# A hybrid encoder block on one core: a sum of squares moves to VectorE, a read-out goes ahead of a product, a down product starts by tile pairs, and two first loads change queues

## The chip, the core and the metric

The kernel runs on one core of a Trainium2 chip. The core has five engines, each with an instruction stream of its own that it works off in order: TensorE (PE) multiplies matrices and writes to the PSUM banks, VectorE (DVE), ScalarE (ACT) and GpSimd (POOL) work element by element, and SyncE (SP) issues loads and stores. ACT issues some of the loads too. Engines wait for one another through semaphores. The metric is the time of one execution on the device in microseconds (us). Of several runs the median counts.

## What is computed

One layer with 1024 tokens of width 1024, float32:

```python
h = rms_norm(x, norm1_g[l])
z = h @ w_in[l]
a, gate, q, k, v = jnp.split(z, splits, axis=-1)
conv_out = conformer_conv(a, gate, dw_kernel[l], dw_bias[l], conv_ln_g[l], conv_ln_b[l])
...
attn_out = neighbourhood_attention(q, k, v, rpb[l])
mix = jnp.concatenate([conv_out, attn_out], axis=-1)
x = x + mix @ w_out[l]
h = rms_norm(x, norm2_g[l])
x = x + (jax.nn.silu(h @ w_gate[l]) * (h @ w_up[l])) @ w_down[l]
```

`conformer_conv` multiplies `a` by the sigmoid of `gate`, runs a 31-tap convolution over positions for each of 512 channels, normalises over the channels (mean, then the mean of the squared deviations, which is the sum of squares in the change) and applies silu. The neighbourhood attention has 8 heads of 64. The inner width of the last line is 2816.

## The kernel before

**Precision.** Every large product is made of three matmuls: each operand is split into a rounded part (`hi`, a cast on ACT) and the remainder (`lo`, a subtraction on DVE or POOL; `split`, L107 to L113), and `mac` (L115 to L119) adds hi x hi, hi x lo and lo x hi into one PSUM bank. L117, L118 and L119 of the profile are these three; they work on 512 columns mostly.

**Order.** The schedule is written out by hand: each engine executes its instructions in the order in which the code records them. PE's products are recorded one by one; `weave` (L127) is called after a product and records the next waiting piece of side work, so a number in `slots` (L1012) says after how many products a piece stands in the streams.

**First loads (L243 to L266).** `chunks` is the list of weight pieces to load; `issue` (L142) issues the next one on SP. The first piece is `wk0`, 128 x 1024, in two halves: the first is loaded by ACT (L258), the second by the first call of `issue`. The token tiles `xt00` to `xt03` (two blocks of 128 rows by 512 tokens each) are loaded in two halves of tokens, FIRST and SECOND, by `load_xt` (L244). ACT's queue holds wk0's first half, xt00's SECOND half and `par` (small parameters); SP's holds xa, xt00's FIRST half, wk0's second half, xt01's FIRST half, wk1 and so on. A load's data is cast by ACT and split by DVE before PE reads it. The products z of the first four token tiles run over these weights: `first_two` (L581) takes wk0's two blocks for tiles 0 and 1, first block, then second, then tiles 2 and 3 follow, which need xt00's SECOND half, then wk1.

**The convolution's normalisation (L890 to L937).** For each half h of the tokens: `conv_mean` sums over channels on PE; `conv_dev` subtracts the mean from the four channel blocks on DVE (L899), squares each on ACT (L901), adds the first two squares on POOL (L903) and the other two and then the sums on DVE (L904, L905); `conv_var` transposes that sum on PE (L910), reduces it on DVE (L911), takes the root on ACT (L912) and the reciprocal on DVE (L913); `conv_rows` spreads the result over the partitions; `conv_norm` (L930) and `conv_silu` make the normalised blocks `cm` (with a `split`, L113), which PE's output projection reads as `pj<-cm`. The pieces of the second half (h = 1) stand at slots 4 (deviation), 13 (variance), 18 and 19, woven into the attention part of the output projection.

**Gate and up (L1300 to L1500).** For each of 22 blocks i of the inner width, gate and up for both halves of the tokens are computed together by a 2 x 2 block scheme with seven products m1 to m7 in place of eight. Each ends in a PSUM bank, and `evac` (L1348) reads it out. Gate's silu for the first half of the tokens is `sl`; for the second half it is left in the bank `D` by m4's read-out (`gate2`, L1340). Two products finish up: m3's read-out adds m3 to the rest (L1369), multiplies the sum with `sl` (L1370) and stores it (`keep`); for the second half, `up2` (L1344) multiplies bank D with up's other sum (L1345) and stores that. `up2` waits in the list `late` after m4 and is recorded behind the read-out of the next product, which is m3 (L1493). Bank D comes from a pool of two banks, so the D of the next block cannot be written before `up2` has read an older one. Some of the blocks' m1 and m2 are themselves split in four by the same scheme (`part`); their banks are q40, q41 and q42 in the rows below.

**Down (L1509 to L1596).** The same scheme for the last product: `SEQ` (L1402) gives the order m1, m2, m6, m5, m7, m3, m4, each over 11 blocks k of the inner width and four tiles t of 128 output columns. m6 and m5 use the banks GB (B0d, B1d, and two halves of a larger tile that both read B2d in the profile), and m5 goes on adding where m6 ended. After the last k of m6 each tile is read out on DVE by `finish` (L1546), tiles 2 and 3 last. Operands of a block (`op`) are prepared four blocks ahead by `prep_item`: two casts on ACT, two subtractions on DVE; one buffer holds two blocks.

Of the kernel before, what the change touches and what calls it, by code (L numbers as in the profile page):

```python
# [9 lines left out]
OP = mybir.AluOpType  # L10
# [61 lines left out]
def build(ctx, tc, a):  # L72
# [66 lines left out]
    def want(src, name, dst, sub=(pool,)):  # L139
        chunks.append((src, name, dst, sub))  # L140

    def issue():  # L142
        if pos[0] < len(chunks):
            src, name, _, _ = chunks[pos[0]]
            if pos[0] not in raws:
                raws[pos[0]] = R(name + "r")
            d = raws[pos[0]]
            if len(src.shape) == 3:
                d = d.rearrange("p (k m) -> p k m", k=src.shape[1])
            sl = slice(512 if name == "wk0" else 0, None)  # L150
            nc.sync.dma_start(d[:, sl], src[:, sl])
            pos[0] += 1

    def take(n=1, ahead=True):
# [86 lines left out]
        x_t[t] = G(f"x{t}")  # L241
        nc.sync.dma_start(x_t[t], a["x"][t * P:(t + 1) * P, :])

    def load_xt(h, kp, sl, queue=None):  # L244
# [3 lines left out]
        (queue or nc.sync).dma_start(xr[h, kp][:, ks, sl], a["xt"][h, kp][:, ks, sl])  # L248

    xr[0, 0] = G("xt00").rearrange("p (k s) -> p k s", s=512)  # L250
    raws[0] = R("wk0r")
# [4 lines left out]
    xa = ST("xa")[:, :258]  # L256
    nc.sync.dma_start(xa, a["xa"])
    nc.scalar.dma_start(raws[0][:, :512], chunks[0][0][:, :512])  # L258
    load_xt(0, 0, SECOND, nc.scalar)
    nc.scalar.dma_start(par, a["par"])  # L260
    for kp in range(4):
        load_xt(0, kp, FIRST)
        if kp < 3:
            issue()
        if kp > 0:
            load_xt(0, kp, SECOND)  # L266
    g1 = par[:, 0:8]
    dwk = par[:, 8:132].rearrange("p (c t) -> p c t", t=CW)
    dwb, lng, lnb = par[:, 132:136], par[:, 136:140], par[:, 140:144]
# [625 lines left out]
    def conv_dev(h):  # L895
        sq = []
        for c in range(4):
            w = of(c, h)
            dve.scalar_tensor_tensor(w, cw["m", h], -1.0 / 512, w, OP.mult, OP.add)  # L899
            sq.append(ST(f"sd{h}{c}"))  # L900
            act.activation(sq[c], w, AF.Square)  # L901
            if c == 1:
                pool.tensor_tensor(sq[0], sq[0], sq[1], OP.add)  # L903
        dve.tensor_tensor(sq[2], sq[2], sq[3], OP.add)  # L904
        dve.tensor_tensor(sq[0], sq[0], sq[2], OP.add)  # L905
        cw["s", h] = sq[0]
# [47 lines left out]
    for i in range(4, 32, 2):  # L954
# [31 lines left out]
        if jobs:  # L986
# [23 lines left out]

    cm += [half(f"cm{h}") for h in range(2)]
    slots = {0: lambda: (weigh(31), evac_hi(7), evac_lo(7)), 3: lambda: conv_var(0),  # L1012
             4: lambda: (conv_mean(1), conv_dev(1)), 6: lambda: (conv_rows(0), conv_norm(0, 0)), 13: lambda: conv_var(1),
             18: lambda: conv_rows(1),
             19: lambda: (act.activation(warm, eps, AF.Silu), [conv_norm(0, c) for c in (1, 2, 3)],
                          conv_silu(0, 0), conv_norm(1, 0))}
# [331 lines left out]
    def evac(i, p, acc):  # L1348
        if p == "m1":
            gt[i] = G(f"g{i}")  # L1350
        l, r = lr(gt[i])
        if p == "m1":
            act.copy(l, acc)
        elif p == "m6":
            u2[i] = ST(f"u2{i}")
            dve.tensor_tensor(u2[i], acc, l, OP.add)
            if i < 2:
                gate2(i, bank[i, "D"])
        elif p == "m2":
            sl[i] = ST(f"sl{i}") if i < 4 else acc  # L1360
            if parted(i, "m1"):
                dve.tensor_tensor(acc, acc, l, OP.add)
            act.activation(sl[i], acc, AF.Silu)
        elif p in ("m5", "m7"):
            dve.tensor_tensor(r, acc, l if p == "m7" else r, OP.add)  # L1365
            if i < 2 and p == "m5":
                up2(i, r, bank[i, "D"])
        elif p == "m3":
            dve.tensor_tensor(l, acc, l, OP.add)  # L1369
            dve.tensor_tensor(l, sl[i], l, OP.mult)  # L1370
            keep(i, 0, l)
        elif i > 1:
            gate2(i, acc)
            late.append(lambda: up2(i, r, acc))
# [110 lines left out]
    for n, (i, p) in enumerate(products):  # L1485
        if n == 1:
            woven.extend([lambda: token_sums(1), lambda: None, lambda: None, lambda: token_rows(1)])
        pacc = product(i, p)
        evac(i, p, pacc)
        if n in after:  # L1490
            after[n]()
        if late and p != "m4":
            late.pop(0)()  # L1493
        due = extra and p in ("m2", "m5", "m7", "m6", "m3")[:5 if parted(i, "m2") else 4]
        if due and not parted(i, "m1"):
            extra.pop(0)()
# [12 lines left out]
        if i == FB - 1 and p in ("m5", "m4", "m3"):  # L1509
            prep_items(1 + (p == "m5"))  # L1510
# [103 lines left out]
```

## Time and profile before

| | |
|---|---|
| runs | 1020.76, 1021.34, 1021.4 us, median 1021.34 |
| the profiled execution | 1020.85 us, of which 1018.9 is the span from its first to its last instruction |
| DVE busy | 782.1 us, 77% of the span |
| ACT busy | 476.5 us, 47% |
| POOL busy | 458.4 us, 45% |
| TensorE's granted clock | 1.0 throughout |
| chain of waits that ended last | TensorE 96%, DVE 1%, POOL 1% |

The profile gives for each engine when an instruction began and how long it took. A row of the time line reads: start, duration, engine, line of the kernel, operation, output <- inputs by the program's names, shapes, count of instructions merged into the row, and in brackets how long the engine had been idle before and what ended that. PE overlaps its matmuls, so their durations overlap too and the distance between two starts is what one costs. The waits of an engine are listed as: who waited <- for whom, total us, times, longest.

### The profile page before, as it was taken

What the parts mean: (1) busy time and instruction counts of PE and PEld (TensorE: products, weight loads), DVE (VectorE), ACT (ScalarE), POOL (GpSimd) and SP (SyncE); (2) the same over time, 40 slices, a digit from 0 to 9 for tenths busy, and PEclk for the clock granted to TensorE, in tenths of its full rate; (3) what the DMA queues carried; (4) which work ended last, traced back from release to release, by engine and by line L of the source; (5) the groups of instructions that cost most, each with busy time, mean ns of one, the idle gap of its engine ahead of it and who ended that gap; (6) DMA issues with size and microseconds to landing.
All of it is one profiled execution on the core that took longest, in us unless ns stands there. A gap on an engine that the chain in (4) does not pass through costs nothing.

```text
span 1018.9 us, 15107 instructions
## 1 busy us (share of the span) xinstructions
PE 1013.9 (100%) x5258; PEld 848.2 (83%) x5258; DVE 782.1 (77%) x1227; ACT 476.5 (47%) x1042; POOL 458.4 (45%) x386
## 2 busy tenths in 40 slices
PE   9999999999999999999999999999999999999998
PEld 8888888877788888888888888888888888888887
DVE  5788997896768476988887787777777766768874
ACT  7556357837877245433433343343332443443432
POOL 1036684535663466266556567566665200003200
PEclk9999999999999999999999999999999999999999
DMA  9416682236503620124334344343341796634631
GB/s 351 169 49 221 204 241 85 96 109 211 179 23 134 238 94 32 58 99 153 137 118 150 126 141 137 119 153 125 135 134 63 255 364 233 211 104 134 213 119 42
DMA packets 75756, 151.70 MB, mean 149 GB/s; under 512 B 14472, under 2 KB 23560, under 8 KB 75040
## 3 DMA queue, kind: packets, MB, share of 16 engines
q1 hardware_dynamic: 73392, 147.12, 42.9%
q10 hardware_dynamic: 2288, 3.62, 1.0%
q8 instruction: 42, 0.69, 0.3%
q14 instruction: 34, 0.28, 0.1%
HBM read 112.06 MB, written 44.11 MB: 153 GB/s over the span
## 4 chain that ended last, share of the span: by engine, by line
PE 96%; DVE 1%; POOL 1%; DMA 0%; ACT 0%; issue 0%; SPq 0%; POOLq 0%; DVEq 0%; ACTq 0%
PE B L117 6%; PE B L118 6%; PE B L119 6%; PE z L117 4%; PE z L119 4%; PE z L118 4%; PE D L117 4%; PE D L118 4%; PE D L119 4%; PE gl L119 3%; PE gl L118 3%; PE gl L117 3%; PE pj L117 3%; PE pj L118 3%; PE pj L119 3%; PE p L779 2%
## 5 line engine op out<-in xcount | busy, mean ns | idle before, releaser
L382 DVE SCALAR_TENSOR_TENSOR cv<-u,par,cv 128x1009 f32<-128x1009 f32 (+14 forms) x92 | 117.5, 1277 | 2.3
L409 POOL TENSOR_TENSOR pa<-pa,pr 128x1022 f32<-128x1022 f32 (+5 forms) x24 | 58.0, 2416 | 38.0 <-ACT pr L408 37.5
L1557 POOL TENSOR_TENSOR ou<-ou,resm 128x512 f32<-128x512 f32 x8 | 12.4, 1553 | 138.4 <-DVE ou L1548 126.1
L109 ACT CAST op<-sr 128x512 fp32r<-128x512 f32 x77 | 47.7, 619 | 57.1 <-PE B2d L119 26.7
L113 DVE TENSOR_TENSOR op<-sr,op 128x512 fp32r<-128x512 f32 x77 | 57.6, 748 | 17.5 <-ACT op L109 17.4
L109 ACT CAST op<-wd 128x512 fp32r<-128x512 f32 x54 | 33.4, 619 | 30.3 <-DVE wd L1452 19.2
L757 ACT ACTIVATE e<-e,mx 128x341 f32<-128x341 f32 (+5 forms) x64 | 35.3, 553 | 18.1 <-DVE mx L752 18.1
L768 POOL TENSOR_SCALAR e<-e,rs 128x341 f32<-128x341 f32 (+5 forms) x64 | 32.9, 528 | 22.1 <-DVE rs L766 21.6
L113 DVE TENSOR_TENSOR op<-wd,op 128x512 fp32r<-128x512 f32 x54 | 40.2, 745 | 1.6 <-ACT op L109 0.4
L1104 DVE TENSOR_TENSOR ts<-gu,ts 128x512 f32<-128x512 f32 x36 | 40.5, 1126 | 0.6
L752 DVE CUSTOM_DVE_ANT_0 e<-s,tab 128x341 f32<-128x341 f32 (+5 forms) x64 | 27.2, 481 | 13.1 <-PE s L735 12.9
L1365 DVE TENSOR_TENSOR g<-D,g 128x512 f32<-128x512 f32 x22 | 15.2, 689 | 23.0 <-PE D L119 23.0
L436 ACT ACTIVATE sq<-z,r 128x64 f32<-128x64 f32 x96 | 28.3, 330 | 5.1 <-PE z L119 5.1
L1342 ACT ACTIVATE D<-D 128x512 f32<-128x512 f32 x22 | 12.8, 582 | 35.7 <-DVE D L1341 35.7
L408 ACT ACTIVATE pr<-u,par 128x1022 f32<-128x1022 f32 (+5 forms) x24 | 27.0, 1137 | 1.6 <-ACT vs L466 1.6
L117 PE MATMUL B2d<-op 128*128 128x512 f32 x66 | 25.8, 391 | 0.0
L119 PE MATMUL B2d<-op 128*128 128x512 f32 x66 | 25.7, 390 | 0.0
L118 PE MATMUL B2d<-op 128*128 128x512 f32 x66 | 25.7, 389 | 0.0
L779 PEld LDWEIGHTS p<-ident,e 128*128 128x128 f32 (+1 forms) x184 | 19.7, 135 | 6.7 <-POOL e L768 5.1
L1058 POOL TENSOR_TENSOR sq<-sq,sq 128x512 f32<-128x512 f32 x12 | 17.6, 1468 | 16.5 <-ACT sq L1054 16.3
L779 PE MATMUL p<-ident,e 128*128 128x128 f32 (+1 forms) x184 | 23.9, 277 | 0.0
L735 PE MATMUL s<-kT,qT 64*128 64x341 f32 (+5 forms) x128 | 21.6, 452 | 0.2
(1492 smaller groups left out, 3752.9 us busy)
## 6 DMA issues: line engine op xcount, KB each, us to landing
gu<-in_gu SPq DMA_DIRECT2D x44, 512.0 KB
sr<-sd SPq DMA_DIRECT2D x77, 256.0 KB
sd<-sd SPq DMA_DIRECT2D x22, 512.0 KB
wd<-in_wd SPq DMA_DIRECT2D x36, 256.0 KB
sd<-g SPq DMA_DIRECT2D x33, 256.0 KB
x<-in_x SPq DMA_DIRECT2D x8, 512.0 KB
xT<-in_xp SPq DMA_DIRECT2D x8, 512.0 KB
xd<-xT SPq DMA_DIRECT2D x16, 256.0 KB
```

The lines of the kernel that those rows point to most:

```text
L109: act.copy(hi, src)
L113: eng.tensor_tensor(*[w[..., sl] for w in (lo, src, hi.bitcast(F32))], OP.subtract)
L117: pe.matmul(acc, lh, rh, start=start, stop=False, skip_group_check=True)
L118: pe.matmul(acc, lh, rl, start=False, stop=False, skip_group_check=True)
L119: pe.matmul(acc, ll, rh, start=False, stop=stop, skip_group_check=True)
L382: dve.scalar_tensor_tensor(acc[:, o], uc[:, i], dwk[:, c, t:t + 1], acc[:, o], OP.mult, OP.add)
L409: pool.tensor_tensor(pa[:, o], pa[:, o], pr[:, o], OP.add)
L436: act.activation(sq[:, h * HD:(h + 1) * HD], z[:, h * HD:(h + 1) * HD], AF.Square, scale=r, accum_out=ss[:, h:h + 1])
L757: act.activation(e, e, AF.Exp, bias=mx.pop((i, hh)), scale=-1.0, accum_out=sums[i][:, hh:hh + 1])
L768: pool.tensor_scalar(es[i][:, hh], es[i][:, hh], rs[:, hh:hh + 1], 1.0, op0=OP.mult, op1=OP.mult)
L779: pe.transpose(pt[:m, g * P:(g + 1) * P], et[i][:, hh, k.start:k.start + m], ident)
L1104: (pool if (i, n) in ON_POOL else dve).tensor_tensor(o, l, r, OP.subtract)
```

## The change

Four edits.

First loads: `issue` can be given a queue. wk0's second half is issued on ACT, behind the first; xt00's SECOND half is issued on SP, behind its FIRST half.

```diff
-    def issue():
+    def issue(queue=None):
...
-            nc.sync.dma_start(d[:, sl], src[:, sl])
+            (queue or nc.sync).dma_start(d[:, sl], src[:, sl])
...
     nc.scalar.dma_start(raws[0][:, :512], chunks[0][0][:, :512])
-    load_xt(0, 0, SECOND, nc.scalar)
+    issue(nc.scalar)
     nc.scalar.dma_start(par, a["par"])
     for kp in range(4):
         load_xt(0, kp, FIRST)
-        if kp < 3:
+        if 0 < kp < 3:
             issue()
-        if kp > 0:
-            load_xt(0, kp, SECOND)
+        load_xt(0, kp, SECOND)
```

Convolution: for the second half of the tokens the first two squares are added on DVE instead of POOL, after all four deviations, and the variance stands at slot 12 instead of 13.

```diff
-            if c == 1:
+            if (h, c) == (0, 1):
                 pool.tensor_tensor(sq[0], sq[0], sq[1], OP.add)
+        if h == 1:
+            dve.tensor_tensor(sq[0], sq[0], sq[1], OP.add)
         dve.tensor_tensor(sq[2], sq[2], sq[3], OP.add)
         dve.tensor_tensor(sq[0], sq[0], sq[2], OP.add)
...
-             4: lambda: (conv_mean(1), conv_dev(1)), 6: lambda: (conv_rows(0), conv_norm(0, 0)), 13: lambda: conv_var(1),
+             4: lambda: (conv_mean(1), conv_dev(1)), 6: lambda: (conv_rows(0), conv_norm(0, 0)), 12: lambda: conv_var(1),
```

Gate and up: m3's product with the gate, and its store, go to the end of `late`, and the whole list is recorded at once, so `up2` comes first.

```diff
         elif p == "m3":
             dve.tensor_tensor(l, acc, l, OP.add)
-            dve.tensor_tensor(l, sl[i], l, OP.mult)
-            keep(i, 0, l)
+            late.append(lambda: (dve.tensor_tensor(l, sl[i], l, OP.mult), keep(i, 0, l)))
...
-        if late and p != "m4":
+        while late and p != "m4":
             late.pop(0)()
```

Down: m5's first two blocks k run on tiles 0 and 1 first, then on tiles 2 and 3.

```diff
-            n = s * QF + k
-            for t in range(4):
-                down(n, t)
+            ahead = p == "m5" and k < 2
+            for k_, t in [(k_, t) for k_ in (0, 1) for t in (2 * k, 2 * k + 1)] if ahead else [(k, t) for t in range(4)]:
+                down(s * QF + k_, t)
```

What the streams hold before and after, at three places. Lines behind L143 are numbered one or two differently after the change. DVE in the convolution's second half (mr1 is the mean, u0 to u3 the channel blocks, sd10 to sd13 their squares), before and then after:

```order
L899 SCALAR_TENSOR_TENSOR u3_1306<-mr1_3339,u3_1306 128x512
L904 TENSOR_TENSOR sd12_3350<-sd12_3350,sd13_3353 128x512
L905 TENSOR_TENSOR sd10_3343<-sd10_3343,sd12_3350 128x512
L930 TENSOR_TENSOR cn00_3368<-u0_538,vr0_3363 128x512
L911 TENSOR_REDUCE cv1_3394<-vs1_3393 128x4
```

```order
L898 SCALAR_TENSOR_TENSOR u3_1306<-mr1_3339,u3_1306 128x512
L904 TENSOR_TENSOR sd10_3343<-sd10_3343,sd11_3346 128x512
L905 TENSOR_TENSOR sd12_3349<-sd12_3349,sd13_3352 128x512
L906 TENSOR_TENSOR sd10_3343<-sd10_3343,sd12_3349 128x512
L931 TENSOR_TENSOR cn00_3368<-u0_538,vr0_3363 128x512
L912 TENSOR_REDUCE cv1_3391<-vs1_3390 128x4
```

DVE has one add more, ahead of its other two; POOL's stream lost it, behind the four splits of wo02.

DVE around m3 of block 2 (B2 and D2 are banks, g2 holds up's sums, sl2 the gate, u23 belongs to block 3), before and then after:

```order
L1341 TENSOR_TENSOR D2_4425<-D2_4425,u22_4409 128x512
L1225 TENSOR_TENSOR qu4m1_4502<-q41m1_4511,qu4m1_4502 128x256
L1369 TENSOR_TENSOR g2_4106<-B2_4396,g2_4106 128x512
L1370 TENSOR_TENSOR g2_4106<-sl2_4161,g2_4106 128x512
L1345 TENSOR_TENSOR g2_4106<-D2_4425,g2_4106 128x512
L1356 TENSOR_TENSOR u23_4562<-B3_4549,g3_4134 128x512
```

```order
L1342 TENSOR_TENSOR D2_4425<-D2_4425,u22_4409 128x512
L1226 TENSOR_TENSOR qu4m1_4502<-q41m1_4511,qu4m1_4502 128x256
L1370 TENSOR_TENSOR g2_4106<-B2_4396,g2_4106 128x512
L1346 TENSOR_TENSOR g2_4106<-D2_4425,g2_4106 128x512
L1371 TENSOR_TENSOR g2_4106<-sl2_4161,g2_4106 128x512
L1357 TENSOR_TENSOR u23_4562<-B3_4549,g3_4134 128x512
```

The read-out of bank D and the product with sl2 have changed places. The same holds for every block from 2 on.

PE at the start of m5 (op32's second half is the first block, op34's first half the second), after the change:

```order
L119 MATMUL B1d_7815<-op32_8425 128x512
L117 MATMUL B0d_7814<-op34_8462 128x512
L118 MATMUL B0d_7814<-op34_8462 128x512
L119 MATMUL B0d_7814<-op34_8462 128x512
L117 MATMUL B1d_7815<-op34_8462 128x512
L118 MATMUL B1d_7815<-op34_8462 128x512
L119 MATMUL B1d_7815<-op34_8462 128x512
L117 MATMUL B2d_7816<-op32_8425 128x512
```

The second block's products on B0d and B1d now stand ahead of the first block's on B2d; before, B2d<-op32 followed B1d<-op32 directly.

More of the change, by code (lines that the diff above doesn't have):

```diff
@@ L242, in load_x, with load_xt @@
         nc.sync.dma_start(x_t[t], a["x"][t * P:(t + 1) * P, :])
-    def load_xt(h, kp, sl, queue=None):
+    def load_xt(h, kp, sl):
         if (h, kp) not in xr:
@@ L247, in load_xt @@
         ks = slice(1, 2) if (h, kp, sl) == (0, 0, FIRST) else slice(0, 2)
-        (queue or nc.sync).dma_start(xr[h, kp][:, ks, sl], a["xt"][h, kp][:, ks, sl])
+        nc.sync.dma_start(xr[h, kp][:, ks, sl], a["xt"][h, kp][:, ks, sl])
     xr[0, 0] = G("xt00").rearrange("p (k s) -> p k s", s=512)
```

## The prediction

> **What bounds the kernel now.** I read the first part of the page, then the waits of TensorE, and then the time lines of each engine around those waits.
>
> ```profile
> span 1018.9 us, 15107 instructions
> PE 1013.9 (100%) x5258; PEld 848.2 (83%) x5258; DVE 782.1 (77%) x1227; ACT 476.5 (47%) x1042; POOL 458.4 (45%) x386
> PE z L587 <- ACT wkq L109: 0.2, 1, 0.2
> PE pj L118 <- DVE cm L113: 0.2, 1, 0.2
> PE D L117 <- DVE g L1345: 0.2, 1, 0.2
> ```
>
> TensorE (PE) is busy for 1013.9 of 1018.9 us, so nothing that leaves its instruction count alone can win more than a few microseconds, and only where PE waits. PE issues the same 5258 instructions after the change. The waits that are left are three of 0.2 us each, and "busy" hides part of a stall, since a matmul's end is modelled. I therefore measure a stall from start to start: with no wait, matmuls of 512 columns start 0.23 us apart, those of 256 columns 0.12 us (rows below). Whatever stands beyond that is the cost of the wait together with the slow first matmul behind it. Four such places exist, and each edit touches one.
>
> **Part 1, the first loads.**
>
> ```profile
> 1.25 0.62 ACTq L248 DMA_DIRECT2D xt<-in_xt  x1
> ...
> 6.31 0.62 ACT L109 CAST wkq<-wk0r 128x512 fp32r<-128x512 f32 x1 [1.27 <-DMA wk0r<-in_qkv]
> ...
> 1.71 0.44 SPq L151 DMA_DIRECT2D wk0r<-in_qkv  x1
> ...
> 6.14 0.63 PE L590 MATMUL z<-wkq,hT 128*128 128x512 f32 x2
> 6.98 0.50 PE L587 MATMUL z<-wkq,hT 128*128 128x512 f32 x1 [0.22 <-ACT wkq L109]
> 7.32 0.40 PE L588 MATMUL z<-wkq,hT 128*128 128x512 f32 x1
> ...
> 11.41 0.39 PE L118 MATMUL z<-wkq,hT 128*128 128x512 f32 x1
> ...
> 9.95 0.69 DVE L113 TENSOR_TENSOR wkq<-wk1r,wkq 128x512 fp32r<-128x512 f32 x1 [0.91 <-ACT wkq L109]
> ```
>
> The fence holds rows of ACT, SP, PE and DVE, each with its start, its duration and, in brackets, the idle time ahead of it. The second half of wk0 is the third load on SP's queue (issued at 1.71), while the second half of xt00 is the second on ACT's (1.25). ACT had nothing to do for 1.27 us until that half of wk0 arrived at 6.31, and PE's L587 at 6.98 waits for its cast. The last matmul ahead of it started at 6.37 (the second of the L590 pair, 0.23 behind 6.14), so the next two should have started by 6.83 and the second did at 7.32: the place costs **0.49 us**. The change exchanges the two loads. PE stops waiting if the cast ends by 6.55 instead of 6.93, so if the half lands 0.4 us before 6.31. The bounds: it lands no earlier and nothing is won (0), or all 0.49 is; more cannot be, because the matmuls ahead of it do not read that half. I take 0.49, since issuing alone begins 0.46 us earlier (1.71 against 1.25) and one load instead of two stands ahead on its queue. What is late next: xt00's second half, now third on SP's queue, which PE reads only six matmuls (1.4 us) after this cast's. Issuing it takes SP 0.2 us longer than the load it replaces (0.62 against 0.44 in these two rows), so xt01 and wk1 are issued that much later; the bytes ahead of wk1 are the same. PE needs wk1's low part, done by VectorE (DVE) at 10.64 (9.95 + 0.69), at 11.41: 0.77 us of cover, 0.28 of it left once PE comes 0.49 earlier.
>
> The Trainium skill, page "DMA: Bandwidth & Descriptors", section "Issuing engines are not separate DMA queues", says that loads issued from several engines run interleaved on the same 16 DMA engines, and that a second issuing engine saves only the sequencer's issue time. By that rule part 1 could win nothing, and the sum below would be 1.18 us instead of 1.67. No row of the kernel before tells the two apart; what it would do here is rival A.
>
> **Part 2, the convolution's second sum of squares.**
>
> ```profile
> 307.53 2.45 DVE L899 SCALAR_TENSOR_TENSOR u<-mr,u 128x512 f32<-128x512 f32 x4
> 310.74 1.11 DVE L904 TENSOR_TENSOR sd<-sd,sd 128x512 f32<-128x512 f32 x1 [0.76 <-ACT sd L901]
> 313.03 0.69 DVE L905 TENSOR_TENSOR sd<-sd,sd 128x512 f32<-128x512 f32 x1 [1.18 <-POOL sd L903]
> ...
> 314.61 0.69 DVE L911 TENSOR_REDUCE cv<-vs 128x4 f32<-128x512 f32 x1
> ...
> 318.71 0.68 DVE L113 TENSOR_TENSOR cm<-cn,cm 128x512 fp32r<-128x512 f32 x1
> ...
> 308.48 2.82 POOL L113 TENSOR_TENSOR wo02l<-wo02r,wo02h 128x256 fp32r<-128x256 f32 x4 [0.98 <-ACT wo02h L109]
> 311.25 1.74 POOL L903 TENSOR_TENSOR sd<-sd,sd 128x512 f32<-128x512 f32 x1
> ...
> 313.87 0.60 PE L910 MATMUL vs<-ident,sd 128*128 128x128 f32 x4
> ...
> 318.87 0.39 PE L117 MATMUL pj<-cm,wo00h 128*128 128x512 f32 x1
> 319.44 0.50 PE L118 MATMUL pj<-cm,wo00h 128*128 128x512 f32 x1 [0.19 <-DVE cm L113]
> 319.78 0.39 PE L119 MATMUL pj<-cm,wo00l 128*128 128x512 f32 x1
> ```
>
> Here PE waits at 319.44 for the low part of the first conv block (L113, 318.71). Read backwards: that row stands behind three norms on DVE, those behind the reduction L911 at 314.61, that behind the norm that follows L905, and L905 at 313.03 waited for GpSimd's (POOL) add L903, which began only at 311.25 because four splits of wo02 (308.48 to 311.30) stand ahead of it. From 318.87 to 319.78 there are two starts, 0.91 us for 0.46: the place costs **0.45 us**.
>
> The change takes POOL's 1.74 us away and gives DVE one more add. DVE's four deviations end at 309.98 (307.53 + 2.45). The moved add takes 0.69 (L905, alone) to 1.11 us (L904, beside POOL), so it ends by 311.0; the add of the other pair, with the squares ready at 310.7, ends by 311.4 to 312.1; the last by 312.1 to 312.8 instead of 313.72. I take the upper ends, since POOL's splits run until 311.30. The transposes of conv_var(1) now stand one product of three matmuls earlier, 313.19 instead of 313.87, and still find their sum ready. The reduction then follows these transposes, as it does now where DVE is free, near 313.85 instead of 314.61. Everything behind it (square root, three norms, L113) moves by 0.76, and PE needs 0.35 of that (319.44 against 318.87 + 0.23). So all 0.45 us is won, with 0.4 us of cover. Even an add at the 1.11 end costs nothing, as the reduction then waits for PE's transposes. POOL's 1.74 us buys nothing by itself: it idles afterwards.
>
> **Part 3, up's read-out before m3's product.**
>
> ```profile
> 458.51 0.68 DVE L1369 TENSOR_TENSOR g<-B,g 128x512 f32<-128x512 f32 x1
> 459.23 1.62 DVE L1370 TENSOR_TENSOR g<-sl,g 128x512 f32<-128x512 f32 x1
> 460.77 0.68 DVE L1345 TENSOR_TENSOR g<-D,g 128x512 f32<-128x512 f32 x1
> ...
> 461.05 0.28 PE L119 MATMUL q42m<-qT3m,qc4m 128*128 128x256 f32 x1
> 461.50 0.50 PE L117 MATMUL D<-S,t3m 128*128 128x512 f32 x1 [0.18 <-DVE g L1345]
> 461.84 0.40 PE L118 MATMUL D<-S,t3m 128*128 128x512 f32 x1
> ```
>
> DVE runs the add of m3 (L1369), then the product with the gate (L1370, 1.62 us here), then up's read-out of bank D (L1345), which ends at 461.45; PE's next user of that bank starts at 461.50. From 461.05 to 461.84 it takes 0.79 us where 0.12 + 0.23 would do: **0.44 us**. With the read-out second it ends near 459.19 + 0.68 = 459.9, 1.2 us before PE could start at 461.17. The other 21 read-outs stall PE nowhere in the list of waits, so they win nothing. The product now ends 0.68 us later each time. Behind it on DVE stands u's add L1356, which loses nothing, as the sum of the three is the same. What a later product holds is the gate's bank, which ACT overwrites for the next pair; the closest case:
>
> ```profile
> 514.77 0.68 DVE L1345 TENSOR_TENSOR g<-D,g 128x512 f32<-128x512 f32 x1
> ...
> 516.81 0.36 ACT L1223 COPY sl<-q60m 128x256 f32<-128x256 f32 x1
> ```
>
> There the product would end where the read-out ends now, 515.45, 1.36 us ahead of the copy. The store of the product is issued 0.68 us later and read back only in the down stage. So 0.44, bounds 0 to 0.44.
>
> **Part 4, m5 of down by tile pairs.**
>
> ```profile
> 896.71 0.39 PE L119 MATMUL B1d<-op 128*128 128x512 f32 x1
> 897.12 0.50 PE L117 MATMUL B2d<-op 128*128 128x512 f32 x1
> 897.46 0.39 PE L118 MATMUL B2d<-op 128*128 128x512 f32 x1
> ...
> 895.77 1.29 DVE L1546 TENSOR_TENSOR ou<-B2d,om 128x512 f32<-128x512 f32 x2 [0.83 <-PE B2d L119]
> ...
> 898.81 0.62 ACT L109 CAST op<-sr 128x512 fp32r<-128x512 f32 x1 [1.50 <-PE B2d L119]
> ...
> 884.58 0.68 DVE L113 TENSOR_TENSOR op<-wd,op 128x512 fp32r<-128x512 f32 x1
> ```
>
> m6's tiles 2 and 3 are read by DVE from 895.77 on, the second until 897.06, and m5's first matmul on tile 2 waits for that: 896.71 to 897.46 is 0.75 for 0.46, **0.29 us**. With two blocks on tiles 0 and 1 first, tile 2 begins two products (six matmuls, 1.36 us) later, at 898.3, when the read is over. The second block's operands are needed 1.36 us earlier; DVE's last split of them is the row at 884.58, twelve us ahead. The first block's buffer is released 1.0 us later (1.36 less the 0.3 won), so the casts at 898.81 (the next to use it) start near 899.8; their block is PE's sixth of m5, after 909. Nothing lost. Bounds 0 to 0.29.
>
> **The sum.** 0.49 + 0.45 + 0.44 + 0.29 = 1.67 us, off the profiled execution's 1020.85 (span 1018.9 and 1.95 around it): 1019.2. The runs shown are 1020.76, 1021.34 and 1021.4, the profiled one 0.49 below their median; against the median the forecast is **1019.7 us**, 0.16% less. The list of waits holds no other PE wait behind these places, so I count each gain as kept to the end; rival B is the exception I found.
>
> **Rivals.**
> A. *The exchange of loads gains nothing.* Both halves pass the same DMA engines, so the half of wk0 lands when the bytes around it have moved, whichever queue issued it; ACT's cast stays at 6.31 and part 1 is 0. For it: ACT's and SP's second and third loads are issued within 0.46 us, and landing takes 4.6 us (1.71 to 6.31), so issue is a tenth of it. Against: one load fewer stands ahead in its own queue. 1021.34 - 1.18 = 1020.2.
> B. *PE runs into DVE at the end of down's m7.*
>
> ```profile
> 949.31 0.69 DVE L113 TENSOR_TENSOR op<-wd,op 128x512 fp32r<-128x512 f32 x1
> ...
> 951.43 0.39 PE L119 MATMUL A0d<-op 128*128 128x512 f32 x1
> ```
>
> DVE splits m7's last blocks here close ahead of PE. The last block's low weights are ready at 950.00 and PE reads them at 951.43: 1.43 us of cover. If DVE's run does not come earlier with PE, a PE that is 1.67 us ahead waits 0.24, and 0.11 for the slow first matmul (461.50 to 461.84 against 0.23): 1020.0. Against: the run starts from m5's read-outs, which PE releases.
> C. *Slower: wk1 comes late,* because xt00's second half now goes ahead of xt01 and wk1 on SP's queue, in pieces half as long as those of the load that it replaces. PE's read at 11.41 has 0.77 us of cover; from there each microsecond of delay of wk1 is one of PE's. It takes 0.77 + 1.18 = 1.95 us to be slower than before, 4.0 to be so by 0.2%. With wk1 later by 3 us: 1021.34 - 1.18 + 2.23 = 1022.4. For it: wk1 is what ACT and DVE wait for next (DVE 0.91 us before 9.95). Against: the bytes ahead of it are the same.
> D. *The edits free nothing*: another wait ends at the same moment in each place, 1021.3. Against: in each place the next condition was looked up above and is met 0.3 to 12 us earlier.
>
> **How the numbers follow.** Forecast 0.55 (1019.7), A 0.22 (1020.2), B 0.13 (1020.0), C 0.04, D 0.06. A difference of 0.2% (2.04 us, to 1019.3) is about what a measurement of this kernel can tell from no change. The forecast lies 0.37 us short of it, and profiled run and median differ by 0.49, so of its 0.55 I give 0.23 to faster, with 0.03 from A and B together: faster 0.26, slower 0.04, same 0.70. Range: down to all four bounds (1.67 us) from the lowest run, 1019.1, and 0.2 for what four places do to one another: 1018.9. Up to 1021.2, just under D, since C and D together hold only 0.10.
>
> **What would show it.** Right: the cast of wk0's second half at 6.0 or earlier and no PE wait there; the reduction L912 behind PE's transposes near 313.8 and no wait for the first conv block; PE's first D of the next row block right behind q42m; B2d of m5 with no wait. PE's list of waits then holds only its first row. Wrong: the cast still at 6.3 (A), a wait on op near 949 (B), a PE wait near 11 us (C), or a wait of the old length with another releaser (D). The forecast also falls if gains of the early parts vanish before 300 us.

## The result, and the profile after

Over 22 runs each, the changed kernel takes 1019.46 us in the median (1019.06 to 1020.45), the kernel before 1021.06 (1020.56 to 1021.59): a ratio of 0.9985, 95% interval 0.9979 to 0.9992. That is 1.60 us less, against 1.67 forecast (1019.7, in a range of 1018.9 to 1021.2). The interval lies just below 1: a small change, but one that the runs tell from none. The profiled execution took 1019.34 us (span 1017.5, before 1018.9).

First the page of the changed kernel and its list of TensorE's waits:

```profile
span 1017.5 us, 15103 instructions
...
PE 1013.1 (100%) x5258; PEld 847.7 (83%) x5258; DVE 782.9 (77%) x1228; ACT 476.5 (47%) x1042; POOL 457.3 (45%) x385
```
```profile
PE up L278 <- POOL ones L274: 1.1, 1, 1.1
```

Of the four rows in this list before, the first is left, as forecast. The list is not everything, though. The next fence holds rows of the changed kernel's first 12 us, of ACT, then PE, then DVE (start, duration, and in brackets the idle time ahead and its releaser):

```profile
5.31 0.51 ACT L304 ACTIVATE hT<-xt,xa 128x256 fp32r<-128x256 f32 x1 [0.66 <-DMA xt<-in_xt]
5.72 0.60 ACT L109 CAST wkq<-wk0r 128x512 fp32r<-128x512 f32 x1
6.46 0.91 ACT L304 ACTIVATE hT<-xt,xa 128x256 fp32r<-128x256 f32 x2
...
9.61 0.62 ACT L109 CAST wkq<-wk1r 128x512 fp32r<-128x512 f32 x1 [0.77 <-DMA wk1r<-in_qkv]
```
```profile
6.49 0.40 PE L586 MATMUL z<-wkq,hT 128*128 128x512 f32 x1
6.73 0.39 PE L587 MATMUL z<-wkq,hT 128*128 128x512 f32 x1
...
10.61 0.39 PE L117 MATMUL z<-wkq,hT 128*128 128x512 f32 x1
11.01 0.50 PE L118 MATMUL z<-wkq,hT 128*128 128x512 f32 x1
11.35 0.40 PE L119 MATMUL z<-wkq,hT 128*128 128x512 f32 x1
```
```profile
10.27 0.69 DVE L113 TENSOR_TENSOR wkq<-wk1r,wkq 128x512 fp32r<-128x512 f32 x1 [0.90 <-ACT wkq L109]
```

The cast of wk0's second half stands at 5.72 instead of 6.31, and PE's L586 and L587 now start 0.24 us apart at 6.49: the wait is gone, and PE's matmuls here lie 0.59 us ahead of the same ones before, 0.11 of which it had already ahead of this place. But xt00's first half arrives late (its split at 5.31, ahead of it 0.66 us of waiting; 4.54 before), and wk1's cast stands at 9.61, 0.32 later than before. DVE has wk1's low part only at 10.96, and PE, which comes earlier, starts L118 at 11.01, 0.40 us behind L117, and the next one 0.34 behind that: 0.29 us given back, which the list of waits doesn't show. At 14 us 0.22 of the 0.59 is left.

The other three places, in the changed kernel: DVE then PE around the first conv block; DVE then PE around the first D of the row block; PE, then DVE, at the start of m5.

```profile
309.69 1.25 DVE L904 TENSOR_TENSOR sd<-sd,sd 128x512 f32<-128x512 f32 x1
310.86 1.22 DVE L905 TENSOR_TENSOR sd<-sd,sd 128x512 f32<-128x512 f32 x1
312.12 0.69 DVE L906 TENSOR_TENSOR sd<-sd,sd 128x512 f32<-128x512 f32 x1
312.73 1.07 DVE L931 TENSOR_TENSOR cn<-u,vr 128x512 f32<-128x512 f32 x1
313.72 0.68 DVE L912 TENSOR_REDUCE cv<-vs 128x4 f32<-128x512 f32 x1
...
317.81 0.68 DVE L113 TENSOR_TENSOR cm<-cn,cm 128x512 fp32r<-128x512 f32 x1
```
```profile
312.98 0.60 PE L911 MATMUL vs<-ident,sd 128*128 128x128 f32 x4
...
318.68 0.39 PE L117 MATMUL pj<-cm,wo00h 128*128 128x512 f32 x1
318.91 0.40 PE L118 MATMUL pj<-cm,wo00h 128*128 128x512 f32 x1
```
```profile
458.46 0.68 DVE L1346 TENSOR_TENSOR g<-D,g 128x512 f32<-128x512 f32 x1
```
```profile
460.40 0.28 PE L119 MATMUL q42m<-qT3m,qc4m 128*128 128x256 f32 x1
460.52 0.40 PE L117 MATMUL D<-S,t3m 128*128 128x512 f32 x1
460.75 0.40 PE L118 MATMUL D<-S,t3m 128*128 128x512 f32 x1
```
```profile
896.98 0.39 PE L119 MATMUL B1d<-op 128*128 128x512 f32 x1
897.21 0.39 PE L117 MATMUL B2d<-op 128*128 128x512 f32 x1
897.43 0.39 PE L118 MATMUL B2d<-op 128*128 128x512 f32 x1
```
```profile
894.68 1.29 DVE L1546 TENSOR_TENSOR ou<-B2d,om 128x512 f32<-128x512 f32 x2 [0.83 <-PE B2d L119]
```

The transposes of 312.98 find their sum ready at 312.81. Their row ends at 313.58, and the reduction L912 starts at 313.72 with no idle time of DVE ahead of it: what it followed last is DVE's own norm L931, which began 0.99 us earlier. In the kernel before it was the same, 0.97 us from this row to the reduction at 314.61:

```profile
313.64 1.07 DVE L930 TENSOR_TENSOR cn<-u,vr 128x512 f32<-128x512 f32 x1
```

The low part of the conv block (L113) is ready at 318.49, and PE reads it at 318.91, on time. Up's read-out (L1346) ends at 459.14, and D follows q42m after 0.12 us. B2d follows B1d after 0.23 us, long after the read-out that ended at 895.97.

To follow the gain over the span, I subtract the start of each of PE's 5258 matmuls from the start of the same matmul before. This **lead** of the changed kernel is 0.22 us at 14 us and 0.19 just ahead of the conv block, 0.66 behind it, 0.65 and 1.09 around the D at 460 us, 1.09 and 1.41 around m5, and 1.41 at the end. So the steps are +0.47, +0.44 and +0.32 (forecast 0.45, 0.44, 0.29), and +0.22 for all of the first 14 us (forecast 0.49 for the loads).

### The profile page after: what moved, and what is told of

Read it like the earlier page. It is cut to its first block, busy times and chain, and to the rows that moved or that the text cites. A ratio compares the mean times of both kernels' runs of the same rounds, so it can differ in the third digit from the quotient of the medians.

```text
span 1017.5 us, 15103 instructions
## 1 busy us (share of the span) xinstructions
PE 1013.1 (100%) x5258; PEld 847.7 (83%) x5258; DVE 782.9 (77%) x1228; ACT 476.5 (47%) x1042; POOL 457.3 (45%) x385
## 4 chain that ended last, share of the span: by engine, by line
PE 95%; DVE 3%; POOL 1%; ACT 0%; issue 0%; DMA 0%; SPq 0%; DVEq 0%; POOLq 0%
PE B L118 6%; PE B L117 6%; PE B L119 6%; PE D L117 4%; PE D L118 4%; PE D L119 4%; PE z L118 3%; PE z L119 3%; PE z L117 3%; PE pj L117 3%; PE pj L119 3%; PE pj L118 3%; PE gl L119 3%; PE gl L118 3%; PE gl L117 3%; DVE cv L381 3%
## 5 line engine op out<-in xcount | busy, mean ns | idle before, releaser
L113 DVE TENSOR_TENSOR op<-sr,op 128x512 fp32r<-128x512 f32 x77 | 58.5, 760 | 17.6 <-ACT op L109 17.5
L113 DVE TENSOR_TENSOR op<-wd,op 128x512 fp32r<-128x512 f32 x54 | 39.2, 725 | 1.1
L117 PE MATMUL B2d<-op 128*128 128x512 f32 x66 | 25.7, 389 | 0.0
L118 PE MATMUL B2d<-op 128*128 128x512 f32 x66 | 25.7, 389 | 0.0
L1055 ACT ACTIVATE sq<-xT 128x512 f32<-128x512 f32 x16 | 10.0, 632 | 25.3 <-DVE xT L945 25.2
```

Of the source, the lines that this page charges most:

```text
L113: eng.tensor_tensor(*[w[..., sl] for w in (lo, src, hi.bitcast(F32))], OP.subtract)
L117: pe.matmul(acc, lh, rh, start=start, stop=False, skip_group_check=True)
L118: pe.matmul(acc, lh, rl, start=False, stop=False, skip_group_check=True)
```

## The experiments

The chance of one profile could explain the 0.22, so the first four kernels undo one part each; the next four take up the loads; the last four set kernels with and without part 1 beside each other again, and split part 2. Each was timed in 11 runs, beside 33 runs of the kernel before on the same chip, whose medians were 1020.91, 1020.82 and 1020.92 in the three groups. Leads are against the profile of before.

### One part undone at a time

Loads in the old order, the rest as changed:

```diff
-    def load_xt(h, kp, sl):
+    def load_xt(h, kp, sl, queue=None):
...
-        nc.sync.dma_start(xr[h, kp][:, ks, sl], a["xt"][h, kp][:, ks, sl])
+        (queue or nc.sync).dma_start(xr[h, kp][:, ks, sl], a["xt"][h, kp][:, ks, sl])
...
-    issue(nc.scalar)
+    load_xt(0, 0, SECOND, nc.scalar)
...
-        if 0 < kp < 3:
+        if kp < 3:
             issue()
-        load_xt(0, kp, SECOND)
+        if kp > 0:
+            load_xt(0, kp, SECOND)
```

> The changed kernel with part 1 undone: the second half of wk0 third on SP's queue again, the second half of xt00 second on ACT's; the other three parts stay. Theory T1 (the exchange wins 0.49 us at wk0's second half, and a wait for wk1 gives about 0.3 of it back, because wk1 lands later behind it): ACT's cast of wk0's second half stands near 6.3 us again with PE's wait at 6.98, the cast of wk1's first half near 9.3, PE without a wait near 11 us; from 13 us on PE is 0.2 us behind the changed kernel, and the time is 1019.7. Rival T2 (the wait for wk1 is a chance of the one profiled run, not of the exchange): the casts of wk1 scatter between 9.3 and 9.6 with either order of loads, and the time is 0.5 us up, 1019.95. Rival A: casts of wk0's second half where the changed kernel has them, 1019.5.

Measured: 1019.51 us (1019.38 to 1020.04), ratio 0.9987 [0.9978, 0.9996]. The cast of wk0's second half is back at 6.11 and PE waits for it (0.3 us in the list of waits), yet the lead at 14 us is 0.19, as good as the changed kernel's 0.22, and at the end it is 1.36. wk1 was cast at 8.49 here, 0.8 earlier than in the kernel before with the same order: landings scatter (T2's claim), but they didn't make this kernel 0.5 us slower. T1's time, 1019.7, is nearer than T2's; only the time of rival A (1019.5) fits, and its rows don't.

The conv edit undone (sd's first pair on POOL, slot 13):

```diff
-            if (h, c) == (0, 1):
+            if c == 1:
                 pool.tensor_tensor(sq[0], sq[0], sq[1], OP.add)
-        if h == 1:
-            dve.tensor_tensor(sq[0], sq[0], sq[1], OP.add)
...
-12: lambda: conv_var(1)
+13: lambda: conv_var(1)
```

> The changed kernel with part 2 undone (GpSimd adds the first pair of squares in both halves, the variance one slot later). Theory: PE waits again for the low part of the first conv block (0.45 us, from start to start), DVE's second add waits for GpSimd's about 1.2 us, PE is 0.45 us behind the changed kernel from 320 us on and keeps that to the end: 1019.9. Rival: the loss is taken up by a later wait that the changed kernel has and this one then does not, 1019.5.

The gate's product ahead of the read-out again:

```diff
-            late.append(lambda: (dve.tensor_tensor(l, sl[i], l, OP.mult), keep(i, 0, l)))
+            dve.tensor_tensor(l, sl[i], l, OP.mult)
+            keep(i, 0, l)
...
-        while late and p != "m4":
+        if late and p != "m4":
```

> The changed kernel with part 3 undone (product with the gate ahead of up's read-out). Theory: PE's first matmul into D of the row block near 460 us waits again, 0.44 us from start to start, nowhere else among the 22 read-outs; 0.44 us up, 1019.9. Rival: in the changed kernel the shift by the earlier parts alone (PE 1.1 us ahead by then) decides, and the undone order costs another amount: up to 1 us if DVE does not come earlier with PE, 0 if it does by more.

And m5 tile by tile as before:

```diff
-            ahead = p == "m5" and k < 2
+            ahead = False
```

> The changed kernel with part 4 undone (m5 of down begins with one block on all four tiles). Theory: PE waits for the read-out of m6's tile 2 again, 0.29 us from start to start, near 896 us: 1019.75. Rival: ACT's casts and DVE's splits behind m5's first block move too, and PE loses or wins as much again at the end of m7, near 949 us: 1019.5 or 1020.0.

The medians are 1020.34 (ratio 0.9993 [0.9984, 1.0001]), 1020.40 (0.9995 [0.9986, 1.0004]) and 1020.16 (0.9992 [0.9983, 1.0001]): each slower than expected by 0.4 to 0.5. The rows of PE at the three places, one kernel each, say what the places themselves cost:

```profile
319.95 0.39 PE L117 MATMUL pj<-cm,wo00h 128*128 128x512 f32 x1
320.50 0.50 PE L118 MATMUL pj<-cm,wo00h 128*128 128x512 f32 x1 [0.16 <-DVE cm L113]
320.83 0.39 PE L119 MATMUL pj<-cm,wo00l 128*128 128x512 f32 x1
```
```profile
461.09 0.28 PE L119 MATMUL q42m<-qT3m,qc4m 128*128 128x256 f32 x1
461.55 0.50 PE L117 MATMUL D<-S,t3m 128*128 128x512 f32 x1 [0.18 <-DVE g L1346]
461.89 0.39 PE L118 MATMUL D<-S,t3m 128*128 128x512 f32 x1
```
```profile
896.09 0.39 PE L119 MATMUL B1d<-op 128*128 128x512 f32 x1
896.50 0.50 PE L117 MATMUL B2d<-op 128*128 128x512 f32 x1
896.84 0.39 PE L118 MATMUL B2d<-op 128*128 128x512 f32 x1
```

At each place the old stall is back: 0.88 us for 0.46 (0.42), 0.80 for 0.35 (0.45), 0.75 for 0.46 (0.29). Across its own place each kernel's lead stays (0.03, -0.01 and 0.00 us), and across the other two it rises by 0.47, 0.44 and 0.31 or 0.32, as in the changed kernel. So the three gains are separate and add up, and nothing later takes them back: the rivals in the three expectations fall. The rest of the loss in these three profiles lies in the first 14 us, with leads there of -1.09, -0.50 and -0.31; the next section takes it apart. A profile is one execution, though (1021.19, 1020.49 and 1020.35 us here, the first of them the slowest of its eleven), so it does not account for the medians.

### What the exchange of the loads does

The changed kernel once more, and the kernel before with the exchange alone:

> The changed kernel once more, for the scatter of its first loads. In the four profiles so far that have the new order of loads, wk0's second half was cast at 5.72 to 5.93 us, but the splits of xt00's second half began at 6.46, 8.78, 7.31 and 8.02, and PE stood 0.22 us ahead of the kernel before at 14 us in one and 0.31 to 1.09 behind it in three; the two profiles with the old order were within 0.19 us of each other. Theory S (the exchange turns a wait of fixed length for wk0 into one of changing length for xt00, third on SP's queue): again another landing between 6.4 and 8.8, and runs that spread over 1 us and more, median 1019.5 to 1020.1. Rival F (the first profile is the rule, the three late ones are chance of one chip): PE 0.2 to 0.6 ahead at 14 us, median 1019.4.

> The kernel before with part 1 alone: the two halves exchanged between the queues, nothing else. My forecast's term of 0.49 us: 1020.5. The first profile's net 0.23: 1020.8. Theory S (nothing or a loss on the average, with a wider spread): 1020.9 to 1021.3, and PE at 14 us between 0.2 ahead of and 1.1 behind the kernel before.

The repeat gave 1019.99 us (1018.76 to 1020.63), ratio 0.9990 [0.9981, 0.9998]; the exchange alone 1020.95, ratio 1.0002 [0.9994, 1.0011], so it wins nothing that can be seen. Rows of the exchange alone, ACT, the list of PE's waits, and PE:

```profile
5.72 0.60 ACT L109 CAST wkq<-wk0r 128x512 fp32r<-128x512 f32 x1
8.54 0.91 ACT L304 ACTIVATE hT<-xt,xa 128x256 fp32r<-128x256 f32 x2 [2.21 <-DMA xt<-in_xt]
```
```profile
PE z L117 <- ACT hT L304: 0.7, 1, 0.7
```
```profile
9.10 0.50 PE L117 MATMUL z<-wkq,hT 128*128 128x512 f32 x1 [0.66 <-ACT hT L304]
9.44 0.40 PE L118 MATMUL z<-wkq,hT 128*128 128x512 f32 x1
```

wk0's half is early (cast at 5.72), but ACT waits 2.21 us for xt00's second half, until 8.54, and PE for the split of it. The lead at 14 us is -0.84; in the repeat of the changed kernel it was +0.66, the best of all.

The trace also holds sixteen updates of the semaphore of each load, which I read as one from each of the core's 16 DMA engines. A reader starts on the last (before: last update of wk0's half 6.29, ACT's cast 6.31). The table has the last updates in us, and for xt00's second half the middle of the sixteen too; it takes in the four kernels of the next sections that have one of the two orders. To its right the lead at 14 us is split up: "start" is the lead at PE's last matmul ahead of wk0's second half (6.37 us in the kernel before), and the next three columns are what PE wins or loses, against the kernel before, where it begins to read wk0's second half, xt00's second half and wk1. They add up to the lead within 0.01. "Clock" is the moment from which the trace records TensorE's full clock.

```
loads  kernel       xt00 1st  wk0 2nd  xt00 2nd (middle)   wk1 |  start   wk0   xt00    wk1 |  lead  clock
new    changed        5.29      5.50     6.43   (6.06)     9.59 | +0.11  +0.47   0.00  -0.35 | +0.22  4.58
new    again          5.24      5.42     6.78   (6.17)     9.11 | +0.21  +0.44   0.00   0.00 | +0.66  4.29
new    again2         5.01      5.43     6.74   (6.22)     9.41 | -0.26  +0.50   0.00   0.00 | +0.23  5.86
new    u_conv         5.30      5.49     8.76   (6.20)    10.78 |  0.00  +0.48  -1.57   0.00 | -1.09  4.66
new    u_gate         5.37      5.74     7.29   (6.44)     9.37 | -1.01  +0.51   0.00   0.00 | -0.50  7.14
new    u_m5           5.49      5.75     7.99   (6.53)    10.07 | -0.52  +0.48  -0.27   0.00 | -0.31  6.00
new    only_loads     5.29      5.49     8.51   (6.04)    10.56 | -0.28  +0.48  -1.04   0.00 | -0.84  5.99
new    conv_slot13    5.28      5.71     8.44   (6.42)    10.49 | -0.62  +0.49  -0.61   0.00 | -0.75  6.25
old    before         4.51      6.29     6.55   (5.04)     9.27 |  0.00   0.00   0.00   0.00 |  0.00  5.37
old    u_loads        4.50      6.08     6.31   (5.05)     8.47 | +0.32  -0.12   0.00   0.00 | +0.19  4.33
old    u_loads2       4.60      6.67     6.94   (5.15)     9.22 | +0.19  -0.58   0.00   0.00 | -0.39  4.22
old    par_late       4.54      7.29     7.67   (5.15)     9.79 | -0.32  -0.69  -0.02   0.00 | -1.03  6.06
```

Three things stand in the landings. The exchange does bring wk0's half earlier in every profile, to 5.4 to 5.8 from 6.1 or more. It makes xt00's first half 0.4 to 1.0 us later, though that load kept its place in SP's queue: what runs beside it has changed. And xt00's second half, whose middle update stood near 5.1, now has it at 6.0 to 6.5. With either order the last of a load's streams comes up to 2.6 us behind the middle one, in some executions and not in others. With the old order such a lag shows at wk0's half (7.29 in par_late), with the new one at xt00's second (four times above 7.9).

The columns of the lead say what that costs PE. At wk0's place the new order wins 0.44 to 0.51 us in all eight profiles (at most 0.06 of a stall is left there), and with the old order the stall itself changes, from 0.49 in the kernel before to 1.17 in par_late. It is paid at xt00's second half, by 0.27 to 1.57 us in four of the eight and by nothing in the other four, and once at wk1 by 0.35. The start goes mostly with the clock and not with the order: +0.19 to +0.32 where the full clock comes at 4.2 to 4.3, with either order, and -1.01 where it comes at 7.14, though PE's first matmuls begin at 1.05 us in all twelve. So leads of equal mean (-0.30 over the eight, -0.31 over the four) do not show that the orders are equal: without the start the means are 0.00 and -0.35, with standard deviations of 0.57 and 0.34, which is too little to tell them apart. That is left to the runs below.

What the start scatters by can be seen in the kernel with part 3 undone (u_gate), whose loads won all they could (+0.51). Three early PE rows:

```profile
5.84 0.63 PE L587 MATMUL z<-wkq,hT 128*128 128x512 f32 x1
6.27 0.63 PE L586 MATMUL z<-wkq,hT 128*128 128x512 f32 x1
6.70 0.60 PE L587 MATMUL z<-wkq,hT 128*128 128x512 f32 x1
```

Matmuls of 512 columns start 0.43 us apart there, against 0.24 in the changed kernel at 6.49 and 6.73: about half the pace. It lasts until the trace records the full clock, at 7.14, and 0.65 of this profile's -1.01 comes in these rows; the rest is its first matmul of z, 0.36 late. (The clock of 1.0 in the table of the time before holds from 5.37 us on; that trace records no clock ahead of it.) The Trainium skill, page "TensorE: Matmul & The Clock Gate", section "What's actually happening", states that TensorE starts at half its clock and rises after a window of activity that doesn't begin with the kernel, so that the number of slow first matmuls changes from run to run; the trace agrees in the pace and in the change from run to run.

### Can the loads be ordered better?

xt00's second half third on ACT's queue (`load_xt` takes a queue again, as above), and, in another kernel, wk1 on ACT's queue behind par:

```diff
     issue(nc.scalar)
+    load_xt(0, 0, SECOND, nc.scalar)
...
-        load_xt(0, kp, SECOND)
+        if kp > 0:
+            load_xt(0, kp, SECOND)
```

```diff
     nc.scalar.dma_start(par, a["par"])
+    issue(nc.scalar)
...
-        if 0 < kp < 3:
+        if kp == 2:
```

> The changed kernel with xt00's second half third on ACT's queue (behind both halves of wk0, ahead of par) and not on SP's. Theory Q (what counts is how much stands ahead in the same queue: SP's carries pieces of 1 KB more slowly than ACT's of 2 KB while both are at work): xt00's second half is split near 6.4 us, xt01 and wk1 are issued 0.5 us earlier and land earlier, PE waits for neither; PE 0.5 us ahead of the kernel before at 14 us in every look, 1019.2. Rival E (the engines share out the bytes whatever the queue): xt00's second half as late as with the changed kernel, 6.5 to 8.8, the time as there. Rival P: par, now behind it, comes after 8 us and holds the splits from the third column block on: PE 0.5 or more behind, 1020.2.

> The changed kernel with wk1 on ACT's queue behind par, instead of fifth on SP's. Theory Q: wk1 lands before 8.6 us (with the changed kernel it was cast at 9.4 to 10.8), but its pieces of 4 KB now take from xt00's second half on SP's queue, whose split comes at 7.5 or later: PE waits there, 0.3 to 1 us behind the kernel before at 14 us, 1020.2. Rival E: both land as in the changed kernel, and the time is the same within its spread.

ACT's rows, of the first kernel and then of the second:

```profile
7.86 0.91 ACT L306 ACTIVATE hT<-xt,xa 128x256 fp32r<-128x256 f32 x2 [1.65 <-DMA xt<-in_xt]
9.34 0.51 ACT L306 ACTIVATE hT<-xt,par 128x256 fp32r<-128x256 f32 x1 [0.57 <-DMA par<-in_par]
```
```profile
8.40 0.91 ACT L305 ACTIVATE hT<-xt,xa 128x256 fp32r<-128x256 f32 x2 [2.39 <-DMA xt<-in_xt]
...
9.61 0.60 ACT L109 CAST wkq<-wk1r 128x512 fp32r<-128x512 f32 x1
```

The first took 1019.91 us, ratio 0.9991 [0.9982, 1.0000]. xt00's half is split at 7.86, its middle update at 6.79, later than in any profile that has it third on SP's queue; then ACT waits 0.57 us for par. So a place in the queue with the larger pieces didn't help, and theory Q falls. E's landing and time hold. P's late par is seen, but not its price: PE lost 0.41 us at xt00's half and only 0.10 behind it. The second took 1020.87, ratio 1.0000 [0.9991, 1.0009]. wk1 is there at 8.15 by its last update (ACT casts it with no wait), and xt00's half pays: its middle update at 7.79, its split at 8.40, lead -0.69. Here all sixteen streams are late, not one: the 512 KB more on ACT's queue were carried at the cost of SP's. What Q expected of this kernel came, and its price (1020.2) was too low.

Then the exchange and its undoing side by side once more, and the old order (by the edit of u_loads) with par's load behind ACT's first activation:

> The changed kernel with part 1 undone, once more, on the same chip as the changed kernel itself. Theory S (with the new order the slowest of a load's sixteen streams comes 0.3 to 2.3 us behind the others and holds xt00's second half; with the old order the same lag falls into slack): median 1019.5, spread half that of the changed kernel, and 0.1 to 0.5 us faster than it. Rival F (the exchange wins its 0.23 to 0.49 us on most executions): 0.2 to 0.5 us slower than the changed kernel.

> The changed kernel a third time, beside the one with part 1 undone. Theory S: median 1019.6 to 1020.1, spread over 1 us. Rival F: 1019.1 to 1019.4.

```diff
-    nc.scalar.dma_start(par, a["par"])
...
     act.activation(warm, eps, AF.Sqrt)
+    nc.scalar.dma_start(par, a["par"])
```

> The changed kernel with the old order of loads, and par's load issued behind ACT's first activation (about 3.6 us in place of 1.9), so that its 77 KB do not compete with wk0's second half. If bytes on the engines decide when wk0's second half lands, it comes some 0.2 us earlier (cast at 5.9 in place of 6.1 to 6.3), PE's wait there shrinks by as much, par is there by 7.4: 1019.3. If what counts is only wk0's place on its own queue: cast at 6.1 to 6.3 as before, 1019.5. If par comes after 7.5 it holds the splits of the third column block, and the time is 1019.8 or more.

Without the exchange 1019.82 us (ratio 0.9988 [0.9979, 0.9997]), with it 1019.43 (0.9986 [0.9977, 0.9995]): rival F's side, by 0.39, after 0.48 on the other side in the two groups before (1019.51 against 1019.99, on two chips). Together, 44 runs with it have a mean of 1019.63 and a standard deviation of 0.46, 22 without it 1019.66 and 0.25. The exchange is worth nothing that these runs can tell from zero. That it widens the spread, as theory S has it, is not shown: the kernel before, with the old order, has a standard deviation of 0.33 over its 121 runs, and par_late, whose loads stand in the old order too, 0.49. Theory S is also wrong where it has the wait for wk0 of fixed length and the old order faster. The kernel with par moved says nothing on par: its load was issued at 1.97 us in place of 1.90, while ACT's table was still loading, so nothing was moved. It took 1019.84 us, ratio 0.9991 [0.9982, 1.0000], and its profile shows how late the old order's wk0 can land (last table row).

### The slot of the variance

```diff
-12: lambda: conv_var(1)
+13: lambda: conv_var(1)
```

> The changed kernel with conv_var(1) back in slot 13, the add left on VectorE. My prediction's step (the reduction follows PE's transposes, so the add alone moves nothing and the slot is what carries it): the transposes start 0.68 us later than in the changed kernel and the reduction with them, the low part of the first conv block is 0.68 us later, and PE waits for it again, 0.2 to 0.35 us from start to start: 0.3 us behind the changed kernel from 320 us on. Rival (the wait for GpSimd's add is what counted): no wait, no loss.

It took 1020.05 us, ratio 0.9992 [0.9983, 1.0000]. DVE, then PE:

```profile
315.26 0.69 DVE L912 TENSOR_REDUCE cv<-vs 128x4 f32<-128x512 f32 x1 [0.51 <-PE vs L911]
...
319.36 0.69 DVE L113 TENSOR_TENSOR cm<-cn,cm 128x512 fp32r<-128x512 f32 x1
```
```profile
319.63 0.39 PE L117 MATMUL pj<-cm,wo00h 128*128 128x512 f32 x1
320.10 0.50 PE L118 MATMUL pj<-cm,wo00h 128*128 128x512 f32 x1
320.44 0.40 PE L119 MATMUL pj<-cm,wo00l 128*128 128x512 f32 x1
```

Now DVE waits 0.51 us for PE's transposes, and PE waits at 320.10: 0.81 us for 0.46, and the lead rises by 0.09 over the place in place of 0.47. The add on VectorE alone carries a fifth of the gain, and the rest comes with the slot. The slot without the add was not tried; by the rows of the kernel before it should win nothing, since the reduction there stood behind DVE's norm, and that behind the sum that POOL's add held back to 313.72. The reduction has two conditions that end within about 0.1 us of each other, DVE's norm and PE's transposes, so the two edits need each other.

## Why the prediction was right, and where it was not

**What bounds the kernel**: four places at which PE starts late, measured from start to start. All four were where the rows said, and each gave what it cost at its own place.

**Part 1 is mis-sized.** The place gave its 0.49 (0.44 to 0.51 us in all eight profiles), but the term is about zero over the runs. The step that failed is the one behind it: the prediction names what is late next, "xt00's second half, now third on SP's queue, which PE reads only six matmuls (1.4 us) after this cast's", and then gives it no price; a cover is worked out for wk1 alone, with "the bytes ahead of wk1 are the same". The runs showed that half landing at 6.4 to 8.8 us, which cost PE nothing up to 7.3 and 0.27 to 1.57 us from 8.0 on; they showed other loads moved by 0.4 us and more, and a lag of single streams that no single profile prices. Rival A's mechanism is false, since wk0's half did land earlier; its price for part 1, nothing, is what the runs show. The Trainium skill, page "DMA: Bandwidth & Descriptors", section "Issuing engines are not separate DMA queues" (loads of several engines interleave on the same 16 DMA engines), agrees with the sum, since what one load won the others lost, and not with the single load: wk0's half, issued 0.46 us earlier, landed 1.0 us earlier on the average of the table. Rival C, a late wk1, was seen at 11 us with 0.29 us; more often it was xt00.

**Part 2 is right in its gain**, 0.47 for 0.45, and in the slot, with one step off. "Even an add at the 1.11 end costs nothing, as the reduction then waits for PE's transposes" does not hold: the two adds beside POOL's splits took 1.25 and 1.22 us, the last ended at 312.81, and the reduction then followed DVE's own norm, about 0.1 us after the transposes. It cost nothing only because PE had 0.42 us of cover.

**Parts 3 and 4 are right**, 0.44 for 0.44 and 0.32 for 0.29. ACT's casts behind m5 stand at 898.76, with PE 1.09 us ahead by then; without that lead it would be 899.85, forecast 899.8.

**Rival B** fell for the reason given against it. DVE's and PE's rows at the end of m7, after:

```profile
947.85 0.68 DVE L113 TENSOR_TENSOR op<-wd,op 128x512 fp32r<-128x512 f32 x1
```
```profile
950.02 0.39 PE L119 MATMUL A0d<-op 128*128 128x512 f32 x1
```

The low weights are ready at 948.53 and read at 950.02: 1.49 us of cover, 1.43 before, since DVE's run came earlier with PE. **Rival D** is out by the three undone parts.

So the time came out as forecast partly by luck: the three sound terms hold 1.23 of the 1.67, and the changed kernel against the kernel before gave -1.60, -0.83 and -1.49 in three groups of runs. What scatters by as much in the profiles is the first microseconds, loads and clock.

## What to carry to other kernels

Measure a stall from start to start and undo one edit at a time: three gains of 0.3 to 0.5 us were confirmed to 0.03 by the lead at their places, while the medians of the same kernels were off by 0.4 to 0.5. A load that is moved to another queue moves the loads beside it too: price it by the sum over all loads in flight, and by several profiles, never by one. Where a wait is traded for slack on another load, ask how much that load's landing scatters. And split a difference up by the places where it arises before it is put down to one cause: a good part of the scatter ahead of 14 us arose here before PE had read any of the loads that were moved.

## What was not expected of the hardware

The last of the sixteen updates of xt00's second half came 0.4 to 2.6 us behind the middle one (table above). In the profile with part 2 undone it is a single one: xt00's fifteenth update is at 6.43, the sixteenth at 8.76. In the next two loads on that queue one is late by as much again (xt01 7.11 and 9.47, wk1 8.53 and 10.78), as if one stream had stopped once and stayed behind. In the other three late profiles too it is one stream, 0.9 to 2.0 us behind the fifteenth. No packet of that profile's first 10 us took longer than 0.9 us, so no long packet explains it; its cause stays open. A load issued in the same place and moment (xt00's first half, at 1.25) landed at 4.50 to 4.60 with the old order and at 5.01 to 5.49 with the new one.
